# Turning layer 0's expert sums and respreading the side work of a two-layer transformer kernel

## The chip, the cores and the metric

The kernel runs on one core of a Trainium2 chip. The metric is device time in microseconds (us) of one execution, the median of several runs; lower is better. In the profile PE is TensorE (PEld its weight loads), DVE is VectorE, ACT is ScalarE, POOL is GpSimd, and SP is the engine whose queue issues most loads. ACTq, POOLq and SPq are the queues of those engines, which issue transfers in order.

## The reference

Two blocks follow one another on 256 tokens of width 1024, all in float32. The change lies wholly in the second block. It has two layers, and two streams of 256 tokens: the tokens `x` and a context. Each layer is a mixer (projections, attention of `x` over `x` and the context, a pooling branch, a convolution branch, gates) and then an expert stage:

```python
def peer_ffn(x, w_q, sub_keys, u_emb, v_emb):          # per chunk of tokens
    q = (xc @ w_q).reshape(PEER_CHUNK, PEER_HEADS, 2, PEER_HALF)
    s = jnp.einsum('thid,hikd->thik', q, sub_keys)
    s1, i1 = lax.top_k(s[:, :, 0], 16); s2, i2 = lax.top_k(s[:, :, 1], 16)
    ...                                                 # best 16 of the sums: eidx, gate
    hid = jax.nn.gelu(jnp.einsum('td,thkd->thk', xc, u_emb[eidx]))
    return jnp.einsum('thk,thkd->td', gate * hid, v_emb[eidx])

for l in range(2):
    ...                                                 # mixer of x, which reads the context
    h = h + mod[:, 5] * peer_ffn(modulate(rms_norm(h, ...)), ...)
    if l == 0:
        hc = hc + mod_c[5] * peer_ffn(modulate(rms_norm(hc, ...)), ...)
```

There are 128 x 128 = 16384 experts. In the last layer the context is only read: its keys and values enter the attention of `x`.

## The kernel before

**Expert stage of x.** `peer` does the experts' product densely: for each of 128 chunks of 128 experts it multiplies all tokens by the chunk's rows of `u` (`hid`, line 1599), applies the GELU, multiplies by a dense table `G` of gates (`wgt`, line 1625) and adds the product with the chunk's rows of `v` (`vside`, line 1643) to four PSUM banks. `G` is built by `gbuild` (line 1538) from one-hot tables, stored in DRAM, and loaded again for four chunks at a time (tile `gp`, line 1629). `topk` finds the experts first. Layer 1 treats 224 of the 256 tokens in this way (`TD`), and the last 32 with gathered rows (`rows_x`).

A chunk of weights is 128 x 1024 in float32, 512 KB (0.524 MB). Most are split into a high and a low part (`WS.split`, lines 286 to 299: ScalarE writes `wa`, VectorE `wb`) and multiplied in three passes of the fast kind (`mm3`); chunks below `nnat` are used as they are, in eight float32 products (`mm1`), which the profile shows as sixteen records.

`peer` is a generator. Its first part runs `hid` for the chunks below `npre`; their results wait in `gpre` tiles. Then it yields None, then come 130 steps of the main loop: `hid(j)` for j from `npre`, `wgt(j - 1)`, `vside(j - 2)`. `NPRE` holds (`nnat`, `npre`) of the two layers. So the first `npre` chunks of the main loop need no load of `u`.

**Where layer 0's sums lie.** With 256 tokens `vside` has the tokens' weights `W` as stationary operand and 512 columns of `v` as moving one: 12 products per chunk; the sums come out by token. With 224 tokens it has 128 columns of `v` stationary and `W` moving: 24 products per chunk; the sums come out by feature, as the rest of the kernel keeps them. So after layer 0's loop ScalarE copies the banks (line 1690), TensorE transposes them (line 1532) and VectorE adds them to `h` (line 1535), and layer 1's loop adds from PSUM directly (line 1678).

**Expert stage of the context.** Only layer 0 has it. `rows` gathers the chosen rows one by one: 512 steps, each an indirect load of 0.524 MB on POOL's queue and one VectorE pass over 128 x 1024 (lines 1459 and 1469). Its results are needed when layer 1's mixer makes the context's keys and values.

**What runs beside what.** Generators yield a cost, and helpers interleave them by it: `par` keeps shares of progress equal, `lead` advances side generators by so many units for each unit of the main one, `along` runs one step of `rows` per 1/rate units. Through layer 0's `ffn_start` TensorE's order is the order written; from line 1821 on a planner orders all engines, with the program's order as priority. In all cases a tile takes one of 42 buffers of 4 KB per partition (`BUFS`, tag `pg`), and a load waits until the buffer that the planner gave it is free.

The places that the change touches: `ffn_start` begins with 24 steps of `topk` (`SOLO`). In layer 0, `lead` then runs `peer`'s first part at 6 units for each unit of `topk`, and `par` runs `gbuild` (64 units) against it (50 units). In layer 1, `par` alone runs the rest of `topk` and `gbuild` (100) against it (28 x 2.99). `RATE[3]` is the number of context rows per unit along layer 0's main loop, whose steps count 256/50 = 5.12 units. The rows that are left run along layer 1's first projections (`RATE[4]`, 0.3 per unit), and the last of them, at `RATE[5]` units each, at the head of a chain: rows, the sums' addition, the context's norm, keys and values (`kv_ctx`), then attention (`attend`). `par` runs this chain against the branches with equal weights (150 and 150).

Of the kernel before, what the change touches and what calls it, by code (L numbers as in the profile page):

```python
# [15 lines left out]
OP = mybir.AluOpType  # L16
AX = mybir.AxisListType

T = 256
D = 1024  # L20

TD = 224
# [9 lines left out]
BLOCKS = ((0, 1, 16), (1, 2, 8), (2, 3, 5), (3, 4, 4), (4, 5, 3), (5, 8, 2), (8, 16, 1))  # L32
NCAND = 50
STARTS = (0, 16, 24, 29, 33, 36, 38, 40, 42, 43, 44, 45, 46, 47, 48, 49)
NPRE = (20, 24), (20, 28)

EARLY = 6.0, 50.0
SOLO, TG = 24, 100.0
BUFS = dict(pg=42)
WT = "pg"  # L40
# [1 line left out]
SEQ, TY = False, 1.0  # L42
SW, ST = 40.0, 240.0
RLAG, RDEPTH = 20, 4
RATE = 2.0, 0.32, 0.25, 0.45, 0.3, 2.0
RLATE, RX = 150.0, 0.15
GS = 2.0 ** 15
DEPTH, LEAD = 3, 2
DU, LU, DV, LV = 2, 1, 2, 1
# [258 lines left out]
class Ker:  # L308
# [1279 lines left out]
    def peer(s, l, xn, G, eng, eng2, nnat, npre, out, keep=None, NT=T, rows=None):  # L1588

        nc, v, mm = s.nc, s.nc.vector, s.nc.tensor.matmul
        PP = 4
        wu = WS(s, s.ai["pu"][l], eng, depth=DU, lead=LU, whole=range(nnat), tag=WT)
        xh = xl = None
        wv = WS(s, [s.ai["pv"][l, :, j] for j in range(128)], eng, depth=DV, lead=LV)
        gel, Wt, gp = {}, {}, {}

        def hid(j):
            w = wu.get()  # L1600
            bank = s.ps("u")
            if j < nnat:
                s.mm1(bank[:, :NT], w, lambda k: xn.ch(k)[:, :NT])
            else:
                c = lambda k: slice(k * 128, (k + 1) * 128)
                s.mm3(bank[:, :NT], [(w[0][:, c(k)], w[1][:, c(k)], xh.ch(k)[:, :NT], xl.ch(k)[:, :NT])
                                     for k in range(8)], 8)
            g = s.s2([128, NT], "gel") if j >= npre else pre[j // PP][:, j % PP]
            nc.scalar.activation(g, bank[:, :NT], AF.Gelu_apprx_tanh)  # L1609
            gel[j] = g  # L1610
        pre = []
        for j in range(npre):
            if j % PP == 0:
                pre.append(s.pg([128, PP, NT], F32, "gpre"))
            if j == nnat:
                xh, xl = Act(s, F32R, "xh"), Act(s, F32R, "xl")
                for a, h, lo in zip(xn.t, xh.t, xl.t):
                    nc.scalar.copy(h, a)  # L1618
                    v.tensor_tensor(lo, a, h, op=OP.subtract)  # L1619
                del xn, a, h, lo  # L1620
            hid(j)
            yield NT / (75 if j < nnat else 100)
        yield None

        def wgt(j):
            if j % 4 == 0:
                gp.clear()
                gp[0] = s.pg([128, NT // 32, 4, 32], F32, "gp")
                eng2.dma_start(gp[0], G[j // 4][:, :NT // 32])
            g = gel.pop(j)  # L1630
            y = g.rearrange("p (c t) -> p c t", t=32)
            v.tensor_tensor(y, y, gp[0][:, :, j % 4, :], op=OP.mult)  # L1632
            W = s.pg([128, 2, NT], F32R, "W")
            nc.scalar.copy(W[:, 0], g)
            v.tensor_tensor(W[:, 1], g, W[:, 0], op=OP.subtract)  # L1635
            Wt[j] = W

        acc = {}
        for tt in range(2):
            for dh in range(2):  # L1640
                acc[tt, dh] = s.ps("m")

        def vside(j):
            vh, vl = wv.get()
            W = Wt.pop(j)
            if NT < T:
                for d in range(8):
                    c = slice(d * 128, (d + 1) * 128)
                    o = acc[d // 4, d // 2 % 2][:, d % 2 * T:d % 2 * T + NT]

                    mm(o, vh[:, c], W[:, 0], start=j == 0 and d % 2 == 0, stop=False, skip_group_check=True)  # L1651
                    mm(o, vh[:, c], W[:, 1], start=False, stop=False, skip_group_check=True)  # L1652
                    mm(o, vl[:, c], W[:, 0], start=False, stop=j == 127, skip_group_check=True)  # L1653
                return
            for tt in range(NT // 128):
                wh, wl = W[:, 0, tt * 128:(tt + 1) * 128], W[:, 1, tt * 128:(tt + 1) * 128]
                for dh in range(2):
                    c, bank = slice(dh * 512, dh * 512 + 512), acc[tt, dh]
                    mm(bank, wh, vh[:, c], start=j == 0, stop=False)
                    mm(bank, wh, vl[:, c], start=False, stop=False)  # L1660
                    mm(bank, wl, vh[:, c], start=False, stop=j == 127)
        for j in range(130):
            if npre <= j < 128:
                hid(j)
            if 1 <= j <= 128:
                wgt(j - 1)
            if j >= 2:
                vside(j - 2)
            if j == npre:
                pre.clear()  # L1670
            yield NT / 50
        h = s.h_load(s.hd["x"], eng)
        if NT < T:
            rows = rows()
            m5 = s.mod(l, 0, 5)
            for d in range(8):
                x = h.ch(d)[:, :NT]
                v.scalar_tensor_tensor(x, acc[d // 4, d // 2 % 2][:, d % 2 * T:d % 2 * T + NT], m5(d), x,
                                       op0=OP.mult, op1=OP.add)
            bank = s.ps("u")  # L1680
            for d in range(8):
                mm(bank[:, d * 32:d * 32 + 32], rows[0][:, d * 128:(d + 1) * 128], s.C("fold"), start=True, stop=True)
            for d in range(8):
                x = h.ch(d)[:, NT:]
                v.scalar_tensor_tensor(x, bank[:, d * 32:d * 32 + 32], m5(d), x, op0=OP.mult, op1=OP.add)
        for tt in range(2 if NT == T else 0):
            evs = []
            for dh in range(2):
                evs.append(s.s2([128, 512], "pev"))
                nc.scalar.copy(evs[-1], acc[tt, dh])  # L1690
            s.add_ffn(h, l, 0, tt, evs)
        s.dump(f"f{l}0", h)
        s.h_store(h, out, eng)
        if keep is not None:
            keep[0] = h
        yield 1.0
# [21 lines left out]
def drain(g):  # L1718
    for _ in g:
        pass  # L1720
# [9 lines left out]
def chain(*gens):  # L1730
    for g in gens:
        yield from g() if callable(g) else g
# [38 lines left out]
def ffn_start(k, l, rx, ws, G, pe, early, tot, ntc=8):  # L1771


    eng = k.nc.gpsimd
    tk = k.topk(l, rx["xn"], ws, eng, rx, skew=bool(early))
    for i in range(SOLO):
        yield next(tk, None)
    pre = until(pe)
    if not early:
        gb = lambda: k.gbuild(rx, G, k.nc.scalar, ntc, skew=False)  # L1780
        yield from par(k, (chain(tk, gb), TG), (pre, tot))
        return
    yield from lead(tk, (pre, early))
    yield from par(k, (k.gbuild(rx, G, k.nc.scalar, ntc), 64.0), (pre, tot))


def program(k, upto):
    nc, ai, ao = k.nc, k.ai, k.ao
    sy, gp = nc.sync, nc.gpsimd

    with k.tc.manual_schedule(engines={mybir.EngineType.PE}):
        x = [k.h_load(ai["xT"].rearrange("a p k t -> a p (k t)"), sy, "x")]
        k.setup()
        ctx0 = ai["ctxT"].rearrange("a p k t -> a p (k t)")
        hc = [k.h_load(ctx0, sy, "hc")]
        rc, rx = {}, {}
        x3, cn, acc = [], [], []
        b1 = k.b1(x.pop(), sy, x3)
        md = k.mods(0, gp)
        rbc = []  # L1800

        def norm_ctx():
            rbc.append((yield from k.rms(hc[0])))
        drain(par(k, (until(b1), 1.0), (norm_ctx(), 1.0)))
        drain(until(md))
        wc = WS(k, ai["w2"][0], gp, whole=WHOLE)

        def choose():
            yield from k.topk(0, rc["xn"], wc, gp, rc, rows=True)
            cn.append(rc.pop("xn"))  # L1810
        rows = k.rows(cn, acc)
        ws = WS(k, ai["w2"][0], sy, whole=WHOLE)
        ctx = chain(k.mixer(0, 1, ctx0, wc, gp, rc, lambda: [], md, seq=True, h=hc.pop(), rbs=rbc.pop()),
                    lambda: par(k, (choose(), 69.0), (k.mods(1, gp), 26.0)))
        xs = chain(b1, lambda: k.mixer(0, 0, k.hd["x"], ws, sy, rx, lambda: [k.kv_load(sy)], seq=SEQ, h=x3.pop()))
        drain(lead(xs, (chain(ctx, lambda: scaled(rows, RATE[0] / RATE[1])), RATE[0]), (k.setup2(), 0.5)))
        kp = {}
        pe = k.peer(0, rx["xn"], k.G[0], sy, sy, *NPRE[0], k.hd["x"], kp)
        drain(along(ffn_start(k, 0, rx, ws, k.G[0], pe, *EARLY), rows, RATE[2]))
    rx.clear()  # L1820
    drain(along(pe, rows, RATE[3]))
    if upto < 5:
# [17 lines left out]
        return xs  # L1840
    pe = k.peer(1, rx["xn"], k.G[1], sy, sy, *NPRE[1], ao, NT=TD, rows=rest)
    rows = k.rows_x(rx["xn"], xs)
    drain(ffn_start(k, 1, rx, ws, k.G[1], pe, None, NPRE[1][1] * 2.99, ntc=TD // 32))
    rx.clear()
    drain(along(pe, rows, RX))

# [14 lines left out]
```

## Time and profile before

| what | value |
|---|---|
| median of 3 runs | 3633.35 us (3629.66 to 3637.85) |
| profiled execution | 3631.59 us; span of its instructions 3629.5 us |
| busy: PE, DVE, ACT, POOL | 3205.7, 2780.5, 1484.5, 936.3 us |
| moved by DMA | 941.06 MB, mean 259 GB/s |
| mean granted clock of TensorE | 0.937 |
| layer 0's dense product | about 1519 to 2275 us |
| layer 1's mixer | about 2275 to 2774 us |
| layer 1's expert stage | about 2774 to 3625 us |

Times within the profile count from the first instruction. A busy share is an average over stages with different limits, so each stage is read by itself. A PE record is longer than the distance to the next one, as matmuls are pipelined; the distance of their starts is what one costs.

### The profile page before, as it was taken

To read this page: it belongs to the slowest core of one execution; us is meant where nothing else is said; L and a number is where in the kernel's file an instruction comes from. 1 tells how busy PE (TensorE), PEld (TensorE's weight loads), DVE (VectorE), ACT (ScalarE), POOL (GpSimd) and SP (SyncE) were. 2 spreads that over 40 slices of the span, in tenths; PEclk is the share of its full clock that TensorE was granted. 3 is DMA by queue.
4 is the path that set the end of the run, shared out by engine and by line. 5 is a ranking of instruction groups with operands and counts; after the bars stand their busy time and mean duration, and the time that the engine had idled before them with its cause. 6 is when DMAs were issued, how large, how long until landed. Compare 5 with 4: busy or idle time off the path is not lost. (4 is left out here: it accounts for less than half of the span.)

```text
span 3629.5 us, 60668 instructions
## 1 busy us (share of the span) xinstructions
PE 3205.7 (88%) x23160; PEld 2911.8 (80%) x23160; DVE 2780.5 (77%) x5718; ACT 1484.5 (41%) x2788; POOL 936.3 (26%) x831
## 2 busy tenths in 40 slices
PE   7989999878699788679999999768999689999999
PEld 5877999657598777558888888658888589999999
DVE  4375675877899799899889899797575968777655
ACT  3454444314355203424434344334362154444444
POOL 2002112123234301475555555251000003111000
PEclk9989999988799899789999999879999799999999
DMA  8537457657688937999999999775444099888764
GB/s 308 163 123 281 159 162 266 211 208 261 226 280 314 343 123 226 324 419 393 379 369 383 371 387 390 239 278 185 134 126 171 25 295 350 298 284 289 259 217 151
DMA packets 315427, 941.06 MB, mean 259 GB/s; under 512 B 29616, under 2 KB 93136, under 8 KB 315136
## 3 DMA queue, kind: packets, MB, share of 16 engines
q1 hardware_dynamic: 130848, 468.77, 36.3%
q0 software_dynamic: 118816, 432.76, 33.0%
q10 hardware_dynamic: 65472, 35.66, 3.3%
q8 instruction: 181, 2.97, 0.3%
q14 instruction: 110, 0.90, 0.1%
HBM read 893.01 MB, written 43.02 MB: 258 GB/s over the span
## 5 line engine op out<-in xcount | busy, mean ns | idle before, releaser
L297 DVE TENSOR_TENSOR wb<-wr,wa 128x1024 fp32r<-128x1024 f32 x842 | 1010.3, 1222 | 289.8 <-ACT wa L295 267.2
L295 ACT CAST wa<-wr 128x1024 fp32r<-128x1024 f32 x842 | 852.1, 1046 | 87.2 <-DMA wr<-in_w 27.4
L429 PE MATMUL pu<-hnh,wa 128*128 128x256 f32 x2000 | 585.9, 293 | 23.1 <-ACT wa L295 22.7
L431 PE MATMUL pu<-hnh,wb 128*128 128x256 f32 x2000 | 582.0, 291 | 23.2 <-DVE wb L297 23.0
L430 PE MATMUL pu<-hnl,wa 128*128 128x256 f32 x2000 | 579.3, 290 | 1.6 <-DVE hnl L559 1.6
L1447 POOL DMA_INDIRECT row<-in_pu,ridx x256 | 357.4, 1396 | 516.6 <-DVE wb L297 92.3
L429 PE MATMUL pu<-xh,wa 128*128 128x256 f32 (+1 forms) x1728 | 484.1, 280 | 0.9 <-ACT xh L1618 0.9
L430 PE MATMUL pu<-xl,wa 128*128 128x256 f32 (+1 forms) x1728 | 483.3, 280 | 1.5 <-DVE xl L1619 1.5
L1447 POOL DMA_INDIRECT row<-in_pv,ridx x256 | 362.6, 1417 | 466.4 <-DVE wb L297 113.3
L431 PE MATMUL pu<-xh,wb 128*128 128x256 f32 (+1 forms) x1728 | 482.8, 280 | 0.0
L429 PEld LDWEIGHTS pu<-hnh,wa 128*128 128x128 f32 x2000 | 397.3, 199 | 37.5 <-ACT wa L295 25.7
L431 PEld LDWEIGHTS pu<-hnh,wb 128*128 128x128 f32 x2000 | 396.8, 198 | 30.9 <-DVE wb L297 29.2
L430 PEld LDWEIGHTS pu<-hnl,wa 128*128 128x128 f32 x2000 | 397.3, 199 | 2.6 <-DVE hnl L559 2.1
L429 PEld LDWEIGHTS pu<-xh,wa 128*128 128x128 f32 x1728 | 333.3, 193 | 10.3 <-ACT wa L295 4.3
L430 PEld LDWEIGHTS pu<-xl,wa 128*128 128x128 f32 x1728 | 333.2, 193 | 5.2 <-DVE xl L1619 1.8
L431 PEld LDWEIGHTS pu<-xh,wb 128*128 128x128 f32 x1728 | 332.5, 192 | 1.6 <-issue 0.4
L436 PE MATMUL pu<-xn,wr 128*128 128x256 f32 (+1 forms) x1408 | 325.8, 390 | 4.4 <-ACT xn L573 4.4
L1469 DVE SCALAR_TENSOR_TENSOR racc<-row,rwg,racc 128x1024 f32<-128x1024 f32 x254 | 325.9, 1283 | 0.4
L1459 DVE CUSTOM_DVE_ANT_0 row<-row,xr 128x1024 f32<-128x1024 f32 x256 | 311.0, 1221 | 5.6 <-issue 5.2
L436 PEld LDWEIGHTS pu<-xn,wr 128*128 128x128 f32 x1408 | 276.3, 200 | 44.9 <-issue 7.5
L1609 ACT ACTIVATE gel<-pu 128x256 f32<-128x256 f32 (+1 forms) x204 | 75.7, 371 | 566.6 <-PE pu L431 532.6
L1651 PE MATMUL pm<-W,wa 128*128 128x224 f32 x1024 | 276.0, 275 | 1.6 <-ACT wa L295 1.6
(430 smaller groups left out, 6395.3 us busy)
## 6 DMA issues: line engine op xcount, KB each, us to landing
wr<-in_w SPq DMA_DIRECT2D x288, 512.0 KB
wr<-in_pu SPq DMA_DIRECT2D x256, 512.0 KB
wr<-in_pv SPq DMA_DIRECT2D x256, 512.0 KB
wr<-in_w POOLq DMA_DIRECT2D x130, 512.0 KB
wm<-in_wmod POOLq DMA_DIRECT2D x96, 512.0 KB
G<-gt ACTq DMA_DIRECT2D x60, 512.0 KB
gp<-G SPq DMA_DIRECT2D x32, 512.0 KB
gp<-G SPq DMA_DIRECT2D x32, 448.0 KB
```

Of the source, the lines that this page charges most:

```text
L295: nc.scalar.copy(a, r)
L297: nc.vector.tensor_tensor(b, r, a, op=OP.subtract)
L429: mm(out, ah, bh, start=i == 0, stop=False)
L430: mm(out, ah, bl, start=False, stop=False)
L431: mm(out, al, bh, start=False, stop=i == n - 1)
L436: s.nc.tensor.matmul(out, w[:, k * 128:(k + 1) * 128], x(k), start=k == 0, stop=k == 7)
L1447: nc.gpsimd.indirect_dma_start(out=t, out_offset=None, in_=tab[w], in_offset=bass.IndirectOffsetOnAxis(ap=s.ridx[:, tt, i:i + 1], axis=0))
L1459: v.tensor_tensor_reduce(t, t, xr[tt], 1.0, 0.0, OP.mult, OP.add, hid[:, i:i + 1])
L1469: v.scalar_tensor_tensor(out[tt], t, wg[:, i:i + 1], out[tt], op0=OP.mult, op1=OP.add)
L1609: nc.scalar.activation(g, bank[:, :NT], AF.Gelu_apprx_tanh)
L1651: mm(o, vh[:, c], W[:, 0], start=j == 0 and d % 2 == 0, stop=False, skip_group_check=True)
```

## The change

The same helpers run with other numbers, layer 0's sums are laid out as layer 1's, and the first `v` chunks are loaded and split at the end of `peer`'s first part, ahead of its yield of None.

```diff
-NPRE = (20, 24), (20, 28)
-EARLY = 6.0, 50.0
+NPRE = (20, 28), (24, 36)
+EARLY = (6.0, 60.0), (4.0, 75.0)
-RATE = 2.0, 0.32, 0.25, 0.45, 0.3, 2.0
+RATE = 2.0, 0.32, 0.25, 0.42, 0.3, 3.0
 def peer(...):
             hid(j)
             yield NT / (75 if j < nnat else 100)
+        wv.load(DV + 2)
+        wv.split(2)
         yield None
     def vside(j):
-            if NT < T:
-                for d in range(8):
-                    ...
-                return
-            for tt in range(NT // 128):
-                wh, wl = W[:, 0, tt * 128:(tt + 1) * 128], W[:, 1, tt * 128:(tt + 1) * 128]
-                for dh in range(2):
-                    c, bank = slice(dh * 512, dh * 512 + 512), acc[tt, dh]
-                    mm(bank, wh, vh[:, c], start=j == 0, stop=False)
-                    mm(bank, wh, vl[:, c], start=False, stop=False)
-                    mm(bank, wl, vh[:, c], start=False, stop=j == 127)
+            for d in range(8):
+                c = slice(d * 128, (d + 1) * 128)
+                o = acc[d // 4, d // 2 % 2][:, d % 2 * T:d % 2 * T + NT]
+                mm(o, vh[:, c], W[:, 0], start=j == 0 and d % 2 == 0, stop=False, skip_group_check=True)
+                mm(o, vh[:, c], W[:, 1], start=False, stop=False, skip_group_check=True)
+                mm(o, vl[:, c], W[:, 0], start=False, stop=j == 127, skip_group_check=True)
         h = s.h_load(s.hd["x"], eng)
+        m5 = s.mod(l, 0, 5)
+        for d in range(8):
+            x = h.ch(d)[:, :NT]
+            v.scalar_tensor_tensor(x, acc[d // 4, d // 2 % 2][...], m5(d), x, op0=OP.mult, op1=OP.add)
...
-        for tt in range(2 if NT == T else 0):
-            evs = []
-            for dh in range(2):
-                evs.append(s.s2([128, 512], "pev"))
-                nc.scalar.copy(evs[-1], acc[tt, dh])
-            s.add_ffn(h, l, 0, tt, evs)
 def ffn_start(...):
-    tk = k.topk(l, rx["xn"], ws, eng, rx, skew=bool(early))
+    tk = k.topk(l, rx["xn"], ws, eng, rx, skew=l == 0)
-    if not early:
-        gb = lambda: k.gbuild(rx, G, k.nc.scalar, ntc, skew=False)
-        yield from par(k, (chain(tk, gb), TG), (pre, tot))
-        return
     yield from lead(tk, (pre, early))
-    yield from par(k, (k.gbuild(rx, G, k.nc.scalar, ntc), 64.0), (pre, tot))
+    yield from par(k, (k.gbuild(rx, G, k.nc.scalar, ntc, skew=l == 0), 64.0), (pre, tot))
 def program(...):
-        drain(along(ffn_start(k, 0, rx, ws, k.G[0], pe, *EARLY), rows, RATE[2]))
+        drain(along(ffn_start(k, 0, rx, ws, k.G[0], pe, *EARLY[0]), rows, RATE[2]))
-    drain(ffn_start(k, 1, rx, ws, k.G[1], pe, None, NPRE[1][1] * 2.99, ntc=TD // 32))
+    drain(ffn_start(k, 1, rx, ws, k.G[1], pe, *EARLY[1], ntc=TD // 32))
```

## Rows read from the trace of the kernel before

**Rows 1.** Windows by stage: engine busy us (count), PE clock, DMA share, GB/s.

```profile
1382.00:1505.00 123.00, 92.49 (x782) 81.36 (x780) 115.84 (x171) 57.59 (x278) 34.14 (x27) 0.84 0.88 277
1505.00:1520.00 15.00, 0.73 (x2) 0.64 (x3) 3.03 (x9) 2.00 (x4) 6.42 (x7) 0.50 1.05 375
1520.00:1630.00 110.00, 85.17 (x336) 65.93 (x334) 108.95 (x154) 32.81 (x52) 80.11 (x53) 0.87 1.03 419
1630.00:2272.00 642.00, 594.50 (x3660) 532.86 (x3661) 583.74 (x772) 268.29 (x417) 343.33 (x236) 0.98 0.99 382
...
2395.00:2500.00 105.00, 75.67 (x539) 72.23 (x539) 93.22 (x170) 37.97 (x57) 29.71 (x19) 0.83 0.64 211
2500.00:2615.00 115.00, 111.50 (x821) 105.36 (x821) 64.77 (x90) 45.08 (x57) 5.81 (x11) 0.98 0.51 156
2615.00:2710.00 95.00, 92.70 (x740) 83.42 (x739) 66.70 (x151) 58.56 (x122) 0.00 (x0) 1.00 0.36 107
...
2852.00:2884.00 32.00, 1.80 (x6) 1.11 (x7) 30.26 (x167) 4.73 (x14) 0.00 (x0) 0.56 0.00 0
2884.00:2975.00 91.00, 78.46 (x674) 74.67 (x675) 70.61 (x113) 44.88 (x233) 0.00 (x0) 0.87 0.77 236
2975.00:3010.00 35.00, 34.28 (x314) 32.46 (x311) 13.98 (x16) 16.61 (x34) 7.24 (x7) 1.00 0.96 342
3010.00:3090.00 80.00, 77.50 (x684) 76.77 (x685) 74.21 (x125) 36.94 (x60) 24.80 (x19) 1.00 0.96 358
3090.00:3622.00 532.00, 532.00 (x4767) 532.00 (x4766) 358.96 (x456) 258.89 (x395) 50.74 (x40) 1.00 0.75 250
```

**Rows 2.** DMA view of 1700 to 2200 us, layer 0's dense product.

```profile
DMA packets 52027, 189.80 MB, mean 380 GB/s; under 512 B 5776, under 2 KB 5776, under 8 KB 51989
...
q0 software_dynamic: 26349, 95.95, 50.1%
q1 hardware_dynamic: 25640, 93.36, 47.7%
...
gp<-G SPq DMA_DIRECT2D x20, 512.0 KB
```

**Rows 3.** PE timeline: two value-side products, then two projection products.

```profile
1701.05 0.40 PE L1659 MATMUL pm<-wa,W 128*128 128x512 f32 x1
1701.28 0.39 PE L1660 MATMUL pm<-wb,W 128*128 128x512 f32 x1
...
2520.00 0.28 PE L429 MATMUL pu<-hnh,wa 128*128 128x256 f32 x1
2520.12 0.28 PE L430 MATMUL pu<-hnl,wa 128*128 128x256 f32 x1
```

**Rows 4.** Timelines of SP, DVE and PE where layer 0's dense product starts.

```profile
1506.71 0.33 SPq L1629 DMA_DIRECT2D gp<-G  x1
...
1515.40 1.43 DVE L1632 TENSOR_TENSOR gpre<-gpre,gp 128x256 f32<-128x256 f32 x4 [8.09 <-DMA gp<-G]
...
1519.27 2.08 PE L1659 MATMUL pm<-wa,W 128*128 128x512 f32 x4 [17.14 <-ACT wa L295]
```

**Rows 5.** Timeline of DVE where layer 0's dense product ends.

```profile
2276.57 4.23 DVE L1535 SCALAR_TENSOR_TENSOR h<-pu,modT,h 128x128 f32<-128x128 f32 x16
```

**Rows 6.** Lines L1469, L976, L1047 within layer 1's mixer: min/median/max ns, starts.

```profile
L1469 DVE SCALAR_TENSOR_TENSOR racc<-row,rwg,racc x24: 1236/1278/1286, 2399.8 to 2466.2; 128x1024 f32<-128x1024 f32 x24
...
L976 ACT COPY v<-pu x8: 580/587/593, 2365.2 to 2579.1; 128x512 f32<-128x512 f32 x8
...
L1047 DVE TENSOR_REDUCE mx<-pm x32: 670/683/691, 2616.5 to 2701.2; 128x1 f32<-128x512 f32 x32
```

**Rows 7.** Costliest groups: the split of a weight chunk, VectorE's half.

```profile
L297 DVE TENSOR_TENSOR wb<-wr,wa 128x1024 fp32r<-128x1024 f32 x842 | 1010.3, 1222 | 289.8 <-ACT wa L295 267.2
```

**Rows 8.** PE timeline and waits of SP at the start of layer 1's expert stage.

```profile
2952.90 3.24 PE L436 MATMUL pu<-xn,wr 128*128 128x224 f32 x16
...
SPq L282 <- DMA G<-gt: 150.6, 13, 83.9
```

More of the change, by code (lines that the diff above doesn't have):

```diff
@@ L1645, in vside @@
             W = Wt.pop(j)
-            if NT < T:
-                for d in range(8):
[L1648 to L1653, printed above, removed]
-                return
-            for tt in range(NT // 128):
-                wh, wl = W[:, 0, tt * 128:(tt + 1) * 128], W[:, 1, tt * 128:(tt + 1) * 128]
-                for dh in range(2):
-                    c, bank = slice(dh * 512, dh * 512 + 512), acc[tt, dh]
-                    mm(bank, wh, vh[:, c], start=j == 0, stop=False)
-                    mm(bank, wh, vl[:, c], start=False, stop=False)
-                    mm(bank, wl, vh[:, c], start=False, stop=j == 127)
+            for d in range(8):
[4 more added lines that the diff above has]
+                mm(o, vl[:, c], W[:, 0], start=False, stop=j == 127, skip_group_check=True)
         for j in range(130):
@@ L1672, in peer @@
         h = s.h_load(s.hd["x"], eng)
+        m5 = s.mod(l, 0, 5)
+        for d in range(8):
+            x = h.ch(d)[:, :NT]
+            v.scalar_tensor_tensor(x, acc[d // 4, d // 2 % 2][:, d % 2 * T:d % 2 * T + NT], m5(d), x,
+                                   op0=OP.mult, op1=OP.add)
         if NT < T:
             rows = rows()
[L1675 to L1679, printed above, removed]
             bank = s.ps("u")
```

## The prediction

> **What bounds the kernel now.** I read the windows by stage first, since each stage has its own limit; then the DMA view and the timelines of each stage that the change touches.
>
> Layer 0's dense product is held by transfers. From 1630 to 2272 us the DMA share is 0.99 at 382 GB/s, while PE shows 594.50 of 642 us and DVE 583.74 [rows 1]. Its pace: 20 loads of `gp`, each for four chunks, in 500 us are 6.25 us a chunk [rows 2]. PE alone would need 24 projections at 0.12 us and 12 value products at 0.23 us [rows 3], 2.88 + 2.76 = 5.64 us. Bytes per chunk: `u` and `v` 1.049 MB, a quarter of `gp` 0.131, and rows at 0.45 x 5.12 = 2.30 of 0.524 MB = 1.208; together 2.388 MB, which at 382 GB/s are 6.25 us. So the pace is what the bytes give. The reader is to see that DVE and PE stand close below: the gain of fewer bytes is limited.
>
> The first 24 chunks have no projection: from 1520 to 1630 us they take 110 / 24 = 4.6 us each, at 419 GB/s and DVE 108.95 of 110 [rows 1]. Between `G`'s build and the first value product PE idles 17.14 us [rows 4].
>
> In layer 1's mixer the worst stretch is 2395 to 2500 us: DVE 93.22 of 105, PE 75.67, clock 0.83 [rows 1]. There the last 24 accumulations of context rows lie, 1.28 us each [rows 6]. From 2615 to 2710, in the attention, PE is full (92.70 of 95) because branch work lies beside it [rows 1].
>
> In layer 1's expert stage PE does almost nothing from 2852 to 2884 us (1.80 of 32, no transfers, clock 0.56) while DVE ends `topk` [rows 1]. A load of `u` waits 83.9 us for a buffer that the stores of `G` free [rows 8]: the early projections can't come forward. From 3090 on PE is without a gap: 4767 products in 532 us, 0.1116 each [rows 1]. Work taken from there comes off the end one to one.
>
> **The change part by part.**
>
> *A. Layer 0's start: +2.* DVE is the limit of the build of `G` (115.84 of 123 us [rows 1]). `NPRE` adds four split projections: 4 splits at 1.22 us [rows 7] = 4.9. The four yields more (4 x 2.56 units) carry 0.25 x 10.2 = 2.6 rows at 1.28 [rows 6] = 3.3. Two `v` splits come forward: 2.4. Sum +10.6. Given back: `gp` takes 8.7 us from issue to its first use, and 3.9 us later comes the first product, behind the split of `v` [rows 4]; with `v` split before, about 2.5 of the 3.9 go, the rest being `W`'s own steps. Four `v` loads (2.1 MB, 5.6 us at 375 GB/s [rows 1]) are no longer issued beside `gp`; I take 3.5 of the 5.6. The two splits are missing later: 2.4. So 10.6 - 8.4 = +2. Bounds: -6 (all 5.6 and the `G` build hides the splits) and +11 (nothing given back). `lead`'s rate stays 6, so the projections before the build don't move; 60 for 50 keeps their share of the build about as it was (0.82 to 0.85).
>
> *B. Layer 0's dense product: -25.* Rows fall to 0.42 x 5.12 = 2.15 a chunk: 0.081 MB less, 2.307 MB, 6.04 us at 382 GB/s. The turned sums need 24 products at 0.12 for 12 at 0.23: 0.12 us more, so PE's floor is 5.76. It leaves 0.28 us where there were 0.61, so I take 6.12, between 6.04 and 6.25. Chunks without a projection are now 28; without `u` they move 1.782 MB for 1.863, so 4.4 us for 4.6. Before: 24 x 4.6 + 104 x 6.25 = 760. After: 28 x 4.4 + 100 x 6.12 = 735. Bounds: -33 (6.04) and +9 (old pace, 4.6 and 6.25, which is -6, and 128 x 0.12 = 15 on top). The page "TensorE: Matmul & The Clock Gate" of the Trainium skill (section on the gap of back-to-back matmuls) gives N / 2.4 GHz plus about 2.5 ns: 24 x 109.2 less 12 x 215.8 ns is 0.03 us a chunk, 4 us in all, where the rows say 0.12 and 15; the rows are used.
>
> *C. The end of layer 0's sums: -2.* Copies and transposes fall away. The 16 additions start at 2276.57 and take 4.23 us [rows 5]; eight of twice the width can start about 1.4 us earlier and take between 2.1 and 4.2 us. Bounds -3.5 and 0.
>
> *D. Layer 1's mixer: +8.* The rows not done before, 130 x 5.12 x 0.03 = 20 less the 2.6 of A, arrive here: 17. At `RATE[4]` the projections (88 units, counted from the yields, as all units here) take 26 as before, so the chain's head grows from 24 rows at 2 units (48) to 41 at 3 (123), against 151 units of branches. In the pool and gate phases (46 units) 15 rows lie where 23 lay: 8 x 1.28 = -10, as DVE is the limit there; the clock, 0.83 in that stretch, is worth another -2. The later rows (25 x 1.28 = 32 us) fall on 2500 to 2615 us, where DVE has 64.77 of 115 [rows 1]: hidden. The price is lateness: the context's keys start at 123 units instead of 48, so the last part of its values, its norm and the whole attention lie behind the branches' end. The attention needs 92.70 less 16 branch chunks x 2.88 = 47 us of PE, and of DVE 66.70 less 16 x 1.22 = 47; alone it takes between 47 and the 85 us that its maxima span [rows 6], so 0 to 38 are lost; I take 12, nearer the sum of work. From the last copy of the values (2579.1) to the first maximum (2616.5) pass 37 us [rows 6], which branch work filled; most is waiting in line, and I take 10 of 0 to 37. Sum -10 - 2 + 12 + 10 = about +8 by rounding down. Bounds: -26 (PE's 29 idle us of the stretch nearly all back, no loss) and +63.
>
> *E. Layer 1's expert stage: -28.* 24 and 36 for 20 and 28: four native projections more (3.1 us each: sixteen records in 3.24 [rows 8]) and four split ones (24 x 0.1116 = 2.68), 23 us of PE before the first value product. PE's idle time from 2852 to 3010 is 158 less 1.80, 78.46 and 34.3 = 44 us [rows 1]. `lead` at 4 puts 20 units, seven projections, between `topk`'s last steps, ahead of the build's tiles in the program, so their buffers no longer wait for `G`'s stores. I let the 23 us fit and of the 21 left take 8. After that the main loop has eight split projections less on an engine without a gap: 8 x 2.68 = -21. The phase without projections is eight chunks longer at 80 / 28 = 2.86 us [rows 1] instead of 2.68: +1. `skew` keeps its values. Sum -28. Bounds: -40 (all 21 taken) and +2 (nothing fits: +23 - 21).
>
> Sum: +2 - 25 - 2 + 8 - 28 = -45. The profiled execution took 3631.59 us, so 3586.6 after; the median of the runs stands 1.8 above it: 3588.
>
> **The rivals.**
>
> *R1. The dense product keeps its pace.* A chunk group waits for its `gp`, whose way is long because rows fill the other queue; as long as POOL's queue always holds some, fewer rows don't shorten it. For it: both queues move nearly the same, 95.95 and 93.36 MB [rows 2]. Against it: rows per chunk fall below what the SP queue moves, so POOL's must run dry at times. Then B is 28 x 4.6 + 100 x 6.25 - 760 = -6, and the sum -26: 3607. The page "DMA: Bandwidth & Descriptors" of the Trainium skill (section on queues, rings and completion order) states that each DMA engine goes round between the queues that have work, packet by packet; by that rule SP's share is half as long as POOL's queue is not empty, and the near equal megabytes agree.
>
> *R2. The mixer gains as well.* If the attention alone is bound by its 47 us of work and half of the stretch's 29 idle us return, D is -14: 3566. For it: PE and DVE need the same 47. Against it: the chain maximum, exponential, transpose, product of each unit.
>
> *R3. Buffers.* The change doesn't do what it says: `gpre` and the early `v` tiles hold up to eight more of 42 buffers, and the early loads wait as they did [rows 8]. A +10, E -5: sum -14, 3619. With R1 on top it is no change.
>
> *R4, slower.* The context's keys come too late: norm (37) and attention (85) run with nothing beside them. The loss is 37 + 85 - 47 = 75, D = +63, the sum +10: 3643. It decides from D = +53 on. For it: 123 of 151 units pass before the context's first chunk. Against it: TensorE's queue still holds the context's values then.
>
> **How the numbers follow.** Forecast 0.42, R1 0.20, R2 0.15, R3 0.10, R4 0.09, R1 with R3 0.04. About 0.2% (7 us) is what a measurement here tells from no change. Faster: the first four less a little of R3, 0.85; same 0.06 (R1 with R3, the edge of R3 and R4); slower 0.09. The range runs from 3560, below R2's 3566, to 3622, above R3's 3619; beyond it are R4, R1 with R3 and the far half of R2's gains, less than 2 in 10.
>
> **What would show it.** In the profile after: `gp` loads of the dense product every 24.5 us instead of 25.0, its first value product about 1521 and its end near 2255; about 67 instead of 50 row passes after that; PE busy through `topk`'s end in layer 1 and the first value product there about 8 us earlier by its distance from the mixer's end, then 92 projections at the old pace. The attention must span less than 70 us. Wrong it is if the mixer from the sums' end to the expert stage's start grows by over 30 us, or if the dense product's pace stays at 6.25.

## The result and the profile after

The change made the kernel slower: 3653.14 us (median of four runs, 3647.23 to 3656.12) against 3634.61 for the kernel before in the same set (median of four), a ratio of 1.0056 with a 95% interval of 1.0039 to 1.0073. The prediction was 3588, with 0.85 on faster. The profiled execution was the fastest of the four; its span of 3645.1 us is 15.6 above the kernel before's, where the medians differ by 18.5.

The windows by stage of the changed kernel answer to [rows 1] (columns as there):

```profile
1382.00:1541.00 159.00, 110.59 (x880) 98.57 (x878) 123.93 (x179) 63.77 (x280) 44.76 (x32) 0.81 0.79 251
1541.00:1554.00 13.00, 0.00 (x0) 0.00 (x0) 2.44 (x6) 1.77 (x10) 2.08 (x3) 0.50 1.04 344
1554.00:1660.00 106.00, 86.22 (x610) 83.72 (x611) 105.92 (x156) 35.91 (x57) 72.37 (x53) 0.86 1.01 405
1668.00:2287.00 619.00, 574.36 (x4698) 568.99 (x4698) 545.59 (x721) 256.35 (x400) 300.82 (x214) 0.99 0.97 370
2412.00:2535.00 123.00, 104.44 (x790) 102.76 (x791) 111.98 (x172) 43.38 (x62) 41.85 (x30) 0.89 0.76 265
...
2880.00:2911.00 31.00, 15.58 (x79) 14.83 (x78) 29.30 (x163) 7.11 (x19) 0.00 (x0) 0.77 0.08 27
2911.00:3003.00 92.00, 82.35 (x692) 79.60 (x691) 65.81 (x102) 44.36 (x210) 0.00 (x0) 0.93 0.64 201
...
3137.00:3637.00 500.00, 500.00 (x4480) 500.00 (x4479) 333.74 (x421) 238.45 (x365) 45.40 (x36) 1.00 0.73 251
```

The first line is the result. The build of `G` has 8 us more of DVE work (123.93 for 115.84), yet takes 36 us longer; DVE, full before, is idle for 35 us of it. The last line is as forecast: PE without a gap, 500 / 4480 = 0.1116 us a product.

Spans shift by some 10 us from one execution to the next before the changed part is reached, so I compare the lengths of stages, which add up to the span. **Start** ends at the first one-hot tile of layer 0 (L1576). **Build** is from there to the last such tile, and **to v** from there to the first value product; **dense** lasts to the last value product, **mixer** from there to the last step of layer 1's normalisation in front of `topk`, **layer 1** to the end of the span; each is counted from start to start of these instructions. (The expectations below that name 753 or 741 us took the dense product's end at the last product of the first of `vside`'s three lines, 1.8 to 2.2 us earlier where the sums are not turned and 0.2 where they are.) **v1** is the part of layer 1 up to its first value product. All stages are in us, from one profiled execution each; time and ratio are those of the timed runs (the kernel before: 3634.6, then 3635.5, 3633.1 and 3634.4 in three sets of runs, each on another chip).

| kernel | start | build | to v | dense | mixer | v1 | layer 1 | time | ratio (95%) |
|---|---|---|---|---|---|---|---|---|---|
| before | 1376.7 | 121.6 | 142.6 | 755.6 | 498.7 | 237.1 | 855.9 | | |
| after | 1377.2 | 158.8 | 177.2 | 741.6 | 505.3 | 246.5 | 843.8 | 3653.1 | 1.0056 (1.0039 to 1.0073) |
| 1 start 0 undone | 1378.3 | 128.4 | 147.5 | 756.6 | 510.4 | 246.2 | 843.5 | 3632.6 | 1.0004 (0.9988 to 1.0020) |
| 2 no early v | 1384.5 | 150.9 | 169.5 | 748.2 | 506.7 | 247.5 | 844.9 | 3653.3 | 1.0047 (1.0029 to 1.0065) |
| 3 native 0 | 1378.3 | 136.0 | 155.1 | 742.7 | 506.0 | 246.0 | 843.4 | 3631.1 | 0.9989 (0.9977 to 1.0001) |
| 4 turned only | 1382.8 | 119.8 | 142.0 | 769.2 | 499.3 | 236.6 | 855.5 | 3644.1 | 1.0024 (1.0010 to 1.0038) |
| 5 rates only | 1383.2 | 121.6 | 140.4 | 742.9 | 510.2 | 232.7 | 851.6 | 3624.8 | 0.9975 (0.9964 to 0.9986) |
| 6 stores on POOL | 1378.6 | 137.8 | 155.0 | 745.0 | 507.2 | 238.6 | 836.1 | 3623.6 | 0.9977 (0.9965 to 0.9989) |
| 7 native both | 1382.0 | 139.6 | 158.9 | 741.9 | 503.1 | 240.6 | 837.9 | 3623.9 | 0.9969 (0.9955 to 0.9983) |
| 8 before, 40 buffers | 1374.1 | 129.2 | 152.3 | 751.1 | 503.8 | 230.4 | 849.2 | 3632.3 | one run |
| 9 before, stores on POOL | 1379.5 | 121.7 | 143.5 | 753.5 | 500.1 | 219.9 | 839.0 | 3618.6 | 0.9954 (0.9937 to 0.9970) |
| 10 not turned | 1375.6 | 159.3 | 177.9 | 732.4 | 507.6 | 245.1 | 842.4 | 3638.0 | 1.0011 (1.0002 to 1.0021) |
| 11 together | 1379.3 | 130.6 | 149.1 | 733.0 | 508.8 | 229.4 | 826.9 | 3599.7 | 0.9901 (0.9885 to 0.9918) |
| 12 together, no early v | 1379.9 | 125.5 | 146.7 | 735.8 | 501.0 | 230.2 | 827.9 | 3596.3 | 0.9895 (0.9878 to 0.9911) |

Rows with the same code in a stage show its scatter: layer 0's way to v is 155.1 and 158.9 in 3 and 7, the mixer 501.0 to 510.4 with the new rates, v1 232.7 to 237.1 in the three rows with layer 1's code and buffers as before (before, 4, 5). So differences of 3 or 4 us in one stage, in the mixer of up to 9, say nothing. After less before: start and way to v +35.1, dense -14.0, mixer +6.6, layer 1 -12.1; together +15.6 of span.

Where did DVE wait in the longer build? These are the waits of DVE from 1380 to 1555 us (total us, times, longest), of the kernel before

```profile
DVE wb L297 <- ACT wa L295: 8.9, 4, 5.5
```

and of the changed one:

```profile
DVE wb L297 <- ACT wa L295: 31.8, 8, 9.2
```

`wb` is VectorE's half of a weight split. It stands in DVE's queue in front of the next one-hot tiles and needs ACT's half, `wa`. The timelines of ACT and then of DVE in the changed kernel show one such wait:

```profile
1468.14 0.46 ACT L1557 ACTIVATE gt<-pm 128x128 f32<-128x128 f32 x2
1468.58 7.03 ACTq L1564 DMA_DIRECT2D G<-gt  x3
1475.66 0.79 ACT L1557 ACTIVATE gt<-pm 128x128 f32<-128x128 f32 x4 [7.06 <-DMA G<-gt]
1476.30 1.07 ACT L295 CAST wa<-wr 128x1024 fp32r<-128x1024 f32 x1
...
1469.29 1.29 DVE L1578 TENSOR_TENSOR gat<-hot,id 128x1024 f16<-128x1024 f16 x2
1477.40 1.23 DVE L297 TENSOR_TENSOR wb<-wr,wa 128x1024 fp32r<-128x1024 f32 x1 [6.83 <-ACT wa L295]
```

ACT issues the stores of `G` itself, and the issue of three of them holds its queue for 7.03 us. The evictions (ACT's copies of `G`'s products out of PSUM, `gt`) and `wa` come after it, so DVE stands for 6.83 us, and with it the one-hot tiles that PE and ACT need next. Such issues are not counted as busy: that ACT shows 63.77 of 159 us hides it.

But this direct wait is the smaller part. Laid over the issues on ACT, 12.7 of the 31.8 us coincide with one; the other 19 come at second hand. In them ACT works off evictions that had stood, or waits for PE, and `wa` has its place behind. Nine microseconds later in the same two timelines:

```profile
1484.37 0.79 ACT L1557 ACTIVATE gt<-pm 128x128 f32<-128x128 f32 x4 [4.68 <-PE pm L1553]
1485.02 1.07 ACT L295 CAST wa<-wr 128x1024 fp32r<-128x1024 f32 x1
...
1486.12 1.22 DVE L297 TENSOR_TENSOR wb<-wr,wa 128x1024 fp32r<-128x1024 f32 x1 [4.96 <-ACT wa L295]
```

So DVE, PE and ACT stand in a ring, each in order, and the timelines alone don't say how much of the second-hand waiting the stores began. Runs 3, 6 and 9 bear on that.

### The profile page after: what moved, and what is told of

Read it like the earlier page. It is cut to its first block, busy times and chain, and to the rows that moved or that the text cites. A ratio compares the mean times of both kernels' runs of the same rounds, so it can differ in the third digit from the quotient of the medians.

```text
span 3645.1 us, 63678 instructions
## 1 busy us (share of the span) xinstructions
PE 3223.8 (88%) x24648; PEld 3005.0 (82%) x24648; DVE 2772.3 (76%) x5706; ACT 1478.3 (41%) x2780; POOL 907.9 (25%) x831
## 4 chain that ended last, share of the span: by engine, by line
PE 42%; DVE 9%; issue 3%; ACT 2%; DMA 1%; ACTq 1%; POOL 0%; DVEq 0%; POOLq 0%
PE pu L431 7%; PE pu L429 7%; PE pu L430 7%; PE pm L1652 5%; PE pm L1654 5%; PE pm L1653 5%; PE pu L436 2%; DVE racc L1469 2%; DVE wb L297 2%; ACT wa L295 1%; DVE row L1459 1%; ACTq L1564 1%; PE pm L1553 1%; DMA wr<-in_pu 1%; DMA row<-in_pv,ridx 0%
## 5 line engine op out<-in xcount | busy, mean ns | idle before, releaser
L1652 PE MATMUL pm<-W,wa 128*128 128x256 f32 (+1 forms) x2048 | 565.4, 283 | 77.5 <-ACT wa L295 59.4
L1653 PE MATMUL pm<-W,wa 128*128 128x256 f32 (+1 forms) x2048 | 564.4, 282 | 0.0
L1654 PE MATMUL pm<-W,wb 128*128 128x256 f32 (+1 forms) x2048 | 540.3, 283 | 4.7 <-DVE wb L297 4.1
L1447 POOL DMA_INDIRECT row<-in_pv,ridx x256 | 341.3, 1333 | 561.6 <-PE pu L431 154.3
L1652 PEld LDWEIGHTS pm<-W,wa 128*128 128x128 f32 x2048 | 396.1, 195 | 84.3 <-ACT wa L295 65.4
L1653 PEld LDWEIGHTS pm<-W,wa 128*128 128x128 f32 x2048 | 397.1, 195 | 0.1
L1654 PEld LDWEIGHTS pm<-W,wb 128*128 128x128 f32 x2048 | 381.4, 195 | 6.9 <-DVE wb L297 5.8
L436 PE MATMUL pu<-xn,wr 128*128 128x256 f32 (+1 forms) x1472 | 335.3, 386 | 4.4 <-ACT xn L573 4.4
```

The costliest lines, as they stand in the source:

```text
L436: s.nc.tensor.matmul(out, w[:, k * 128:(k + 1) * 128], x(k), start=k == 0, stop=k == 7)
L1447: nc.gpsimd.indirect_dma_start(out=t, out_offset=None, in_=tab[w], in_offset=bass.IndirectOffsetOnAxis(ap=s.ridx[:, tt, i:i + 1], axis=0))
```

## The experiments

No kernel leaves out any of the computation.

**1. Layer 0's start undone**, all else as changed:

```diff
-NPRE = (20, 28), (24, 36)
-EARLY = (6.0, 60.0), (4.0, 75.0)
+NPRE = (20, 24), (24, 36)
+EARLY = (6.0, 50.0), (4.0, 75.0)
```

> The changed kernel with layer 0's start as before the change: NPRE 20, 24 and the rate and total of its lead as before; the early load and split of v stay, and so does all of layer 1. Theory S (the four more split projections stretched the build of G, 122 to 159 us): the build is back at 120 to 126 us, the first value product comes near 1520 us, the dense product takes 741 + 4 x 1.75 = 748 us, and the time is 3653 - 33 + 7 = 3627 us (3620 to 3634). Rival V (the loads and splits of v ahead of the main loop hold buffers that the build wants): the build stays over 145 us and the time above 3645.

Build 128.4, time 3632.6: theory S in the main (the build just above its range). The four projections, with the total that paces them, account for 177.2 - 147.5 = 30 us of the way to v; 5 of the 35 are left with the early `v`. The dense product takes 756.6 and not 748: the four chunks without projection were worth 15 there.

**2. No early v:**

```diff
-        wv.load(DV + 2)
-        wv.split(2)
```

> The changed kernel without the early load and split of v, in both layers. Theory S: the build of layer 0 stays at 150 to 160 us, the way from the last one-hot tile to the first value product grows from 18 to about 22 us, and the time is 3653 to 3662 us. Rival V: the build is back at about 125 us, and the time falls to about 3625.

As S expects, 3653.3. The early load costs 8 us in the build and gives back 7 in the dense product (748.2 to 741.6). Rival V is out as the main cause.

**3. Native form for layer 0's 28 early projections.** They use the weights as loaded, without splits; the parts of the activations are formed after the last one.

```diff
-NPRE = (20, 28), (24, 36)
-EARLY = (6.0, 60.0), (4.0, 75.0)
+NPRE = (28, 28), (24, 36)
+EARLY = (6.0, 67.0), (4.0, 75.0)
...
+        if xh is None:
+            xh, xl = parts(xn)
+            del xn
```

> The changed kernel with all 28 early projections of layer 0 in their native form (NPRE 28, 28; the two parts of the activations are formed after the last of them; the total that paces them 67 for 60, since their units are larger). Eight splits on ACT and DVE and four buffers less in the build; 8 x (3.1 - 2.7) = 3 us more on PE there. Theory S: the build takes 112 to 122 us and the first value product is near 1520, time 3653 - 36 = 3617 us (3608 to 3628). Rival P (the four projections cost TensorE time in the build, in whichever form): the build stays over 145 us, time 3650 to 3660. Rival V as well: it stays over 145.

The way to v falls by 22 us and the time to 3631.1, but the build stays 14 above the kernel before: two thirds of what S promised. P is out, V stays out. The wait for `wa`, as above:

```profile
DVE wb L297 <- ACT wa L295: 14.2, 2, 12.8
```

The issues of the 32 stores add up to 63.8 us on ACT in this build, more than the 49.5 of the changed kernel, and still it is 23 us shorter. So it is not ACT's standing by itself that costs, but what of DVE's work hangs on it.

**4. Turned sums alone, in the kernel before** (`vside` and the eight additions from the changed kernel, the rest as before).

> The kernel before with the turned sums of layer 0 alone (24 products of 256 columns a chunk in place of 12 of 512, and the eight additions without copies and transposes at the end). Theory T (TensorE pays 0.12 us a chunk as its spacing says, and the loop hands it on): the dense product grows by 10 to 15 us, the end of the sums is 3 us shorter, time 3634 + 8 to 12 = 3642 to 3646 us. Rival H (the pace is set by the load queue, which waits for buffers and is not held by TensorE): the dense product stays within 3 us of 753, time 3629 to 3634.

Theory T: dense +13.6, nothing else moves by more than the scatter, time +8.5.

**5. The two rates alone, in the kernel before:**

```diff
-RATE = 2.0, 0.32, 0.25, 0.45, 0.3, 2.0
+RATE = 2.0, 0.32, 0.25, 0.42, 0.3, 3.0
```

> The kernel before with the two rates alone: context rows at 0.42 for 0.45 in layer 0's dense product and at 3 for 2 units in front of layer 1's mixer. What the other runs leave over for it: the dense product 12 to 14 us shorter (753 to 740), with most of the gain in the first 24 chunks, which have no projection; the mixer from the sums' end to the expert stage 5 to 12 us longer; time 3635 - 5 = 3630 us (3622 to 3634). Rival: the load queue's pace doesn't change with fewer rows (its loads wait for buffers), the dense product stays over 748, and the time rises to 3640.

Dense -12.7, mixer +11.5, time -8.3 (this profiled execution lies 5 us above its median, and the mixer is the stage that scatters). The rival fell: the pace with projections goes from 6.316 to 6.192 us a chunk (98 chunks between two activations). My guess on where the gain lies was wrong too: nearly all is in those chunks.

**6. The stores of `G` issued by POOL**, all else as changed (`eng` is POOL in `ffn_start`):

```diff
-    yield from par(k, (k.gbuild(rx, G, k.nc.scalar, ntc, skew=l == 0), 64.0), (pre, tot))
+    yield from par(k, (k.gbuild(rx, G, eng, ntc, skew=l == 0), 64.0), (pre, tot))
```

> The changed kernel with the stores of G issued by POOL in place of ACT, in both layers. Theory Q (ACT stands for 5 to 10 us at each of the eight groups of stores, the splits of the early projections wait behind it, and DVE waits for the splits): layer 0's build shrinks from 159 to under 140 us, the idle time of DVE before its split falls from 32 to under 12 us, time 3630 to 3642. Rival B (the build is slow because buffers are short): the build stays at 150 to 165 us, time 3645 to 3660; it may grow if POOL's stores start late, since they free buffers.

Theory Q in layer 0; the time falls below its range. Waits of DVE, same stretch:

```profile
DVE gpre L1634 <- DMA gp<-G: 9.5, 1, 9.5
DVE racc L1469 <- DMA row<-in_pv,ridx: 6.6, 3, 3.0
DVE row L1459 <- DMA row<-in_pu,ridx: 4.4, 2, 3.9
DVE wb L297 <- ACT wa L295: 2.1, 2, 1.6
```

The wait for `wa` falls from 31.8 to 2.1 us, the way to v by 22.2, the time by 30 to 3623.6 (layer 1 gains 8 of it). What remains is DVE's longer work and 11 us for row gathers, whose issue now shares POOL with the stores. The line L1564 itself, its durations in ns as min/median/max, in the changed kernel

```profile
L1564 ACTq DMA_DIRECT2D G<-gt x32: 366/1248/5072, 1395.4 to 1546.4; - x32
```

and with POOL:

```profile
L1564 POOL DMA_DIRECT2D G<-gt x32: 885/914/967, 1397.0 to 1523.4; - x32
```

The edit moves more than the issue. The queues over the whole program (packets, MB, share of 16 engines' span), in the changed kernel

```profile
q0 software_dynamic: 118816, 432.76, 32.6%
q10 hardware_dynamic: 65472, 35.66, 3.2%
```

and with POOL:

```profile
q0 software_dynamic: 127456, 464.22, 35.2%
q10 hardware_dynamic: 3072, 4.20, 0.4%
```

The 60 stores of both layers, 31.5 MB, go from 62,400 packets to 8,640 in the queue that also brings the rows. Their share of the DMA engines hardly changes (2.6% with POOL for 2.8%), but whether the stores also land sooner, and free buffers sooner, no run separates from the issue.

**7. Native form in layer 1 too** (36, 36 and a total of 79 for 75; otherwise as 3).

> As the kernel with all 28 early projections of layer 0 native, and layer 1's 36 native as well (NPRE 28, 28 and 36, 36; total 79 for 75 there). Theory S for layer 1 (split projections stretch the build there, 112 us for 70): the build falls to 85 to 100 us and the first value product comes 10 to 20 us earlier by its distance from the mixer's end (246 to about 232), time 3612 to 3622. Rival P (TensorE's time is the price there: it is nearly without a gap): native form costs 12 x 0.4 = 5 us more, the distance is 246 to 252, time 3631 to 3638.

Layer 1's build shrinks from 111 to 84 us, the way to its first value product by 5: between the two theories. There the shorter build hardly brings the first value product forward.

**8. The kernel before with 40 buffers for 42.**

> The kernel before with 40 buffers for 42 in the shared pool. If buffers set the pace of layer 0's build (rival B), it grows from 122 to over 130 us, as it grew by 8 us where the early loads of v held two to six of them; and the dense product, whose loads wait for buffers, loses over 5 us. If they don't, both stay within 3 us of 122 and 753.

The build grows by 7.6 us (just under my mark), the way to v by 9.7; the dense product doesn't suffer, and the one time is no worse. Buffers shift the build by some 8 us, as in 2, but they don't set the dense product's pace.

**9. The kernel before with the stores on POOL**, the edit of 6 in both branches of `ffn_start`.

> The kernel before with the stores of G issued by POOL in place of ACT, in both layers, and nothing else. Theory Q (ACT's standing at the stores couples into DVE only through the splits): DVE waits for the splits 9 us in this build before, so it falls from 122 to 112 to 120 us, layer 1's start gains 0 to 8 us, time 3633 - 5 to - 12 = 3621 to 3628. Rival: the gain of the stores on POOL is there only with the changed start; then the time stays within 3 us of 3633.

The time is better than expected, 3618.6, and the build is not: 121.7 as before. DVE's wait for `wa` does fall (8.9 to 2.5 us), but 8.5 us of waits for row gathers take its place:

```profile
DVE row L1459 <- DMA row<-in_pu,ridx: 6.2, 3, 4.9
DVE wb L297 <- ACT wa L295: 2.5, 3, 1.4
DVE racc L1469 <- DMA row<-in_pv,ridx: 2.3, 2, 1.8
```

The whole gain is in layer 1, 17 us (13 to 17 against the three rows with its code as before). The largest waits of SP there from 2840 to 3050 us, in the changed kernel

```profile
SPq L282 <- DMA G<-gt: 101.6, 10, 44.1
SPq L282 <- PE pu L436: 56.0, 4, 29.5
```

and here:

```profile
SPq L282 <- DVE gat L1578: 42.5, 5, 31.9
SPq L282 <- DMA G<-gt: 42.5, 5, 10.0
```

Against the 150.6 us of [rows 8], loads wait 42.5 for stores of `G`; that may be the earlier issue or the larger packets, as in 6. In the kernel before ACT's timeline has this issue and what stood behind it:

```profile
2959.00 8.48 ACTq L1564 DMA_DIRECT2D G<-gt  x2
2967.53 2.31 ACT L1557 ACTIVATE gt<-pm 128x128 f32<-128x128 f32 x13 [8.86 <-issue]
```

**10. Sums not turned**, all else as changed.

> The changed kernel with layer 0's sums as they were (12 products of 512 columns a chunk, copies and transposes at the end). Theory T (the turned form costs TensorE 0.12 us a chunk, which the loop hands on also at the lower rate of rows): the dense product falls from 741 to 725 to 728 us, the sums' end is 1 to 3 us longer, time 3653 - 13 = 3640 us (3634 to 3645). Rival: at the lower rate the loads set the pace and not TensorE; the dense product stays over 736 and the time over 3648.

Theory T, but less than it said: dense -9.2 where 13 to 16 were expected, time -15 (the spans of the two profiled executions differ by 9.2). The window of its chunks with projection has 566.75 us of PE in 610:

```profile
1668.00:2278.00 610.00, 566.75 (x3533) 508.58 (x3532) 545.62 (x720) 256.72 (x400) 300.61 (x214) 0.99 0.98 375
```

Beside the changed kernel's line (574.36 of 619), PE has 7.6 us less and the stretch is 9 shorter; DVE's work is the same. PE is not full in either, and yet its extra time passes through.

**11 and 12. Put together:** 7 with the sums not turned and the stores on POOL; 12 without the early `v` as well.

> What the runs point to, put together: the changed kernel with the sums as before, the early projections native in both layers (28, 28 and 36, 36), and the stores of G on POOL. Terms against the changed kernel's 3653: sums -13, stores -30, native form another -5 to -12 beyond what the stores already give back: 3598 to 3607 us, ratio to the kernel before 0.990 to 0.993. If native form and stores remedy the same wait and nothing more: 3610. If POOL's row gathers, held back by the stores, set the build now: 3615 or more.

> The same without the early load and split of v. From the pair with and without it before: the build 8 us shorter, the dense product 7 us longer, time within 3 us of the other. If buffers no longer hold up the build once the stores are on POOL, the build gains nothing and this one is 3 to 7 us slower.

3599.7 and 3596.3 us, both faster than either kernel. The early `v` is again a wash: 5 us off the build, 3 on the dense product.

## Why the prediction was wrong

**A (+2, measured +35) is the step that failed**: "DVE is the limit of the build of `G`", and so its cost is DVE's added instructions, +10.6 less what comes back. The instructions are about there (8 us). What I left out is that DVE works in order and that its half of each split hangs on ACT, whose queue stands at the stores' issues. With four more splits, spread over the build, DVE waits 31.8 us for `wa` where it waited 8.9: 12.7 directly at an issue, the rest by way of evictions and PE. Runs 1 and 2 put 27 to 30 us on the four projections and 5 to 8 on the early `v`. Runs 3 and 6 each take back 22 by removing one partner of the wait, the splits or the stores on ACT. With the stores on POOL in both kernels the new start costs 155.0 - 143.5 = 11.5 us (6 against 9), near the +10.6 before anything given back; with the stores on ACT it costs 34.6. The trace before had the sign of it, 8.9 us of DVE's waits for `wa`, and the 32 issues on ACT there, which add up to 47 us. That the new start stretches the build this much only with the stores on ACT is shown by 6 and 9. That it is the issue, and not the other packets, is argued from the timelines; and so is why the splits of the kernel before cost so little (9 leaves its build alone): its five splits of `u` lie in 34 us of the build, the nine of the changed kernel in 81.

The handover gained as forecast from `gp`'s issue on. Timeline of the changed kernel, beside [rows 4]:

```profile
1547.81 0.33 SPq L1631 DMA_DIRECT2D gp<-G  x1
...
1553.45 1.43 DVE L1634 TENSOR_TENSOR gpre<-gpre,gp 128x256 f32<-128x256 f32 x4 [4.19 <-DMA gp<-G]
...
1554.36 1.22 PE L1652 MATMUL pm<-W,wa 128*128 128x256 f32 x4 [14.59 <-ACT W L1636]
```

5.6 and 0.9 us where there were 8.7 and 3.9: 6 us. But `gp` is issued 11.9 us after the last one-hot tile where it was 8.4, so from the build's end to the first value product only 2.6 are left (18.4 for 21.0), against the 37 of the build.

**B (-25, measured -14): right in kind, wrong in its sizes.** The lower rate gives -12.7 (run 5), about half of what the bytes promise: 0.12 us a chunk for 0.21. So bytes alone don't set the pace. The turned sums cost 13.6 (4) and 9.2 (10), which I had covered by the transfers: "It leaves 0.28 us where there were 0.61". That margin between averages covered little of it. The 0.12 us from [rows 3] stand above both (128 x 0.12 = 15). The estimate of 4 us by the formula of the page "TensorE: Matmul & The Clock Gate" of the Trainium skill (section "Back-to-back issue gap") lies below both. The four chunks without a projection brought 15 (1 against after) where I had 7, but cost more in front. The DMA view from 1700 to 2200 us, beside [rows 2]:

```profile
q1 hardware_dynamic: 25626, 93.30, 49.1%
q0 software_dynamic: 24588, 89.53, 47.0%
```

Rows moved 6.4 MB less and SP's queue the same. That looks like rival R1 and isn't: run 5 alone speeds SP's queue up (pace 6.192), and the turned sums take it back (6.326). The round-robin rule of the Trainium skill's page "DMA: Bandwidth & Descriptors" (section "Queues, rings and completion order") that stood beside R1 is not refuted by this, but it did not set the pace.

**C and D (+6 together, measured +6.6) hold**, within a scatter as large as the forecast: the ten rows with the new rates average 506.6 us in the mixer, the three with the old ones and 42 buffers 499.4. The additions, beside [rows 5], and the row passes and maxima, beside [rows 6]:

```profile
2297.35 3.21 DVE L1669 SCALAR_TENSOR_TENSOR h<-pm,modT,h 128x256 f32<-128x256 f32 x8
...
L1469 DVE SCALAR_TENSOR_TENSOR racc<-row,rwg,racc x44: 1248/1278/1282, 2296.2 to 2562.0; 128x1024 f32<-128x1024 f32 x44
...
L1047 DVE TENSOR_REDUCE mx<-pm x32: 670/683/692, 2679.7 to 2729.7; 128x1 f32<-128x512 f32 x32
```

67 row passes were left, as forecast (these 44 accumulations and 23 first passes of L1459), and the maxima span 50 us for 85. What that wins, the late keys seem to lose; no run tells the two apart. R2 (-14) and R4 (+63) are both out.

**E (-28, measured -12).** The main loop's -21 came (589.7 us for 611.2 from first to last value product). "I let the 23 us fit" failed: the first value product is 9.4 us later (9 to 14 against the rows before, 4 and 5), not 8 earlier. PE does work through the end of `topk` (15.58 of 31 us for 1.80 of 32), but the build grows from 70 to 112 us, and loads still wait 101.6 us for stores. With the stores on POOL and native form (11) the term is -29. But 9 shows that most of what I meant to win there could be had without the new start: 855.9 to 839.0 from the stores alone, against 836.1 with both (6).

Of the rivals, R3 (buffers) named the right stages, with a third of A's price and another cause (buffers shift the build by some 8 us, runs 2 and 8). None foresaw the wait, and the range ended 31 us short of 3653.

## What to carry to other kernels

Before adding work to a stage that one engine fills, list for each added instruction what it waits for on which other queue, and what that queue may be standing at: issues on ACT's queue don't count as busy in the profile, and here they add up to 47 us of a build in which ACT seemed half idle. Price a split of work over two in-order engines by the chain and not by the fuller engine's instructions. And don't let a margin between averages cover added work: an engine 93% busy in a loop of hand-overs here passed on 9 to 14 us of some 15, although the averages left room.

## What the runs showed of the hardware

The issue of one store of `G` (1,024 pieces of 512 bytes) took ACT 0.37 to 5.07 us in the changed kernel, and POOL 0.89 to 0.97 us for the same stores; in the kernel before the 32 of layer 0 add up to 47.2 us on ACT, with POOL in run 6 to 29.3. The same store crosses the DMA engines as 1,040 packets when ACT issues it and as 144 when POOL does (run 6: 62,400 and 8,640 for 60 stores).

The Trainium skill says on the page "DMA: Bandwidth & Descriptors" (section "Issuing engines are not separate DMA queues") that issuing from several engines saves only the issuing time, which is usually small beside the transfer. A single store here agrees with the second half: its issue on POOL takes 0.91 us in the median, its landing 5.7 (run 6). But the issues add up, 47.2 us of ACT's queue in layer 0, and taking them from ACT was worth 30 us in the changed kernel (6) and 16 in the kernel before (9). With the packets changed as well, no run here shows that the issuing time is all that was saved.
